# Lasting tiles in the rings, and fifteen small loads ahead of the last stores, in a matmul with bias and residual

## The chip, the cores and the metric

The kernel runs on one core of one Trainium2 chip. The metric is the time of one execution in microseconds (us).

## The reference

```python
def setup_inputs():
    batch, m, k, n = 16, 512, 1024, 768
    # x [16,512,1024], weight [1024,768], bias [768], residual [16,512,768], all float32

def reference(x, weight, bias, residual):
    return (np.matmul(x, weight) + bias + residual).astype(np.float32)
```

## The kernel before

The 8192 rows are cut into 64 row tiles of 128 rows, and eight row tiles make a super tile `S`. ACT casts a row tile of x to bf16, PE transposes it and multiplies it by the weights, POOL and DVE add bias and residual into the residual's own tile `ro`, and SP stores `ro`. All large DMAs are issued by SP, in the order of the program: SP stops at a DMA whose semaphores are not there yet, and everything behind it stops too. Buffers come from rings, which here allocate a new tile under an old tag each time:

```python
    def ring(pool, name, i, n, shape, dt):
        return pool.tile(shape, dt, name=name, tag=f"{name}{i % n}", bufs=1)
    ...
    def store(S, j0=0, j1=J, n0=0, nl=N):
        K_(nc.sync.dma_start(
            out=out_d[S, :, j0:j1, n0:n0 + nl], in_=ro[S][:, j0:j1, n0:n0 + nl]
        ))
    ...
    for t in range(HEAD, n_t):            # one row tile
        cast(t + 2)
        S, j = divmod(t, J)
        ...                               # loads of later super tiles, stores of earlier ones
        ...                               # matmuls of t, transposes of t + 1, adds of t - 1
        if S == n_s - 1 and j == 0:
            store(S - 1)                  # 3 MB
        if S == n_s - 1 and j == J // 2:
            store(S, 0, J // 2)           # 1.5 MB
        if S == n_s - 1 and j == J - 2:
            store(S, J // 2, j)           # 0.75 MB
        if S == n_s - 1 and j == J - 1:
            store(S, j - 1, j)            # 0.375 MB
    t, S = n_t - 1, n_s - 1
    for b, (n0, nl) in enumerate(chunks): # the last row tile in two parts
        ...
        store(S, J - 1, J, n0, nl)        # 0.25 and 0.125 MB
```

`S - 1` below always means the super tile before the last, `S - 2` the one before that.

Of the kernel before, what the change touches and what calls it, by code (L numbers as in the profile page):

```python
# [8 lines left out]
FP32 = mybir.dt.float32  # L9
BF16 = mybir.dt.bfloat16  # L10
P = 128
J = 8
HEAD = 3
X_BUFS = 2
RO_BUFS = 4
TMP_BUFS = 4
# [5 lines left out]
def kernel(  # L22
# [8 lines left out]
    nc = tc.nc  # L31
    x2d = x.flatten_outer_dims()
# [3 lines left out]
    N = weight.shape[1]  # L36
    n_c = K // (2 * P)
# [10 lines left out]
    const = ctx.enter_context(tc.tile_pool(name="const", bufs=1))  # L48
    sb = ctx.enter_context(tc.tile_pool(name="sb", bufs=1))
    ps = ctx.enter_context(tc.tile_pool(name="ps", bufs=1, space=bass.MemoryType.PSUM))  # L50

    def ring(pool, name, i, n, shape, dt):
        return pool.tile(shape, dt, name=name, tag=f"{name}{i % n}", bufs=1)

    def psum_o(i):
        return ring(ps, "po", i, HEAD, [P, N], FP32)

    x_sb, ro, xb, xt, po, tmp = {}, {}, {}, {}, {}, {}
    K_ = tc.keep_in_program_order


    def load_x(S, j0=0, j1=J):
        if S < n_s:
            if j0 == 0:
                x_sb[S] = ring(sb, "x_tile", S, X_BUFS, [P, J, K], FP32)
            K_(nc.sync.dma_start(out=x_sb[S][:, j0:j1, :], in_=x_d[S, :, j0:j1, :]))

    def load_res(S, j0=0, j1=J):
        if S < n_s:
            if j0 == 0:  # L70
                ro[S] = ring(sb, "ro", S, RO_BUFS, [P, J, N], FP32)
            K_(nc.sync.dma_start(out=ro[S][:, j0:j1, :], in_=res_d[S, :, j0:j1, :]))
# [4 lines left out]
# [6 lines that stand above are left out]
    def cast(t, engine="act"):  # L83
        if t < n_t:
            xb[t] = ring(sb, "xb", t, 4, [P, K], BF16)
            copy = nc.scalar.copy if engine == "act" else nc.vector.tensor_copy
            K_(copy(out=xb[t], in_=x_sb[t // J][:, t % J, :]))  # L87

    def transp(t):
        if t < n_t:  # L90

            pt = ring(ps, "pt", t, 2, [P, n_c, P], FP32)
            pairs = xb[t][:, :].bitcast(FP32)
            for c in range(n_c):
                K_(nc.tensor.transpose(  # L95
                    out=pt[:, c, :], in_=pairs[:, c * P:(c + 1) * P], identity=ident
                ))
            xt[t] = ring(sb, "xt", t, 4, [P, n_c, P], FP32)
            K_(nc.vector.tensor_copy(out=xt[t], in_=pt))  # L99
# [9 lines left out]
    def mms(t, i):  # L109
        if i == 0:  # L110
            po[t] = psum_o(t)
        for n0, nl in chunks:
            mm(t, i, n0, nl)
# [4 lines left out]
    def pool_add(t):  # L118
        if 0 <= t < n_t:
            r = row(t)  # L120
            K_(nc.gpsimd.tensor_add(out=r, in0=r, in1=tmp[t] if t < EARLY else bias_sb))  # L121

    def finish(t, n0=0, nl=N):
        if t < 0:
            return
        p = po[t][:, n0:n0 + nl]
        if t < EARLY:
            tmp[t] = ring(sb, "tmp", t, TMP_BUFS, [P, N], FP32)
            K_(nc.vector.tensor_add(out=tmp[t], in0=p, in1=bias_sb))  # L129
        else:  # L130
            K_(nc.vector.tensor_add(out=row(t, n0, nl), in0=p, in1=row(t, n0, nl)))  # L131
# [2 lines left out]
    bias_row = ring(sb, "tmp", TMP_BUFS - 1, TMP_BUFS, [P, N], FP32)  # L134
    K_(nc.gpsimd.memset(bias_row, 0.0))  # L135
    K_(nc.scalar.dma_start(out=bias_row[0:1, :], in_=bias[None, :]))
    w_st = ring(sb, "ro", RO_BUFS - 1, RO_BUFS, [P, n_c, 2, N], FP32)
    w_sb = const.tile([P, n_c, 2, N], BF16, name="w_sb")

    load_x(0, 0, 2)  # L140
# [11 lines left out]
    load_x(1, 4, 8)  # L152
    load_res(1)

    warm = const.tile([P, 512], BF16, name="warm")
    K_(nc.vector.memset(warm, 0.0))  # L156
    ones = ring(sb, "tmp", 0, TMP_BUFS, [P, P], FP32)
    K_(nc.vector.memset(ones, 1.0))
    warm_a = const.tile([1, 2], FP32, name="warm_a")
    K_(nc.vector.memset(warm_a, 0.0))  # L160
# [53 lines left out]
    for t in range(HEAD, n_t):  # L214
        cast(t + 2)
        S, j = divmod(t, J)
        if (t + 2) % J == J - 1:
            if S == 0:
                load_x(X_BUFS, 0, J // 2)
                load_x(X_BUFS, J // 2, J)  # L220
            else:
                load_x(S + X_BUFS)
            load_res(S + X_BUFS)
            if 1 <= S < n_s - 1:
                store(S - 1)
        if t < n_t - 1:
            for i in range(len(steps)):
                mms(t, i)
                if i == 0 and t >= n_t - J // 2:
                    finish(t - 1)  # L230
                if i == T_STEP:
                    transp(t + 1)
        if t < n_t - J // 2 or t == n_t - 1:
            finish(t - 1)
        if t - 1 < EARLY:
            pool_add(t - 1)
        if t + 1 >= EARLY:
            pool_add(t + 1)
        if S == n_s - 1 and j == 0:
            store(S - 1)  # L240
        if S == n_s - 1 and j == J // 2:
            store(S, 0, J // 2)
        if S == n_s - 1 and j == J - 2:
            store(S, J // 2, j)
        if S == n_s - 1 and j == J - 1:
            store(S, j - 1, j)
# [37 lines left out]
```

## Time and profile before

| | kernel before |
|---|---|
| time, median of 2 runs | 211.07 us (210.93 to 211.21) |
| span of the profiled run | 209.0 us |
| PE busy | 200.4 us, 96% |
| SP queue's packets, share of 16 DMA engines | 97.9% (87.03 MB) |
| last matmul issued | 202.8 us |
| store of S-1 issued, landed | 182.5, 200.8 us |
| the five last stores issued | 192.5 to 203.5 us |
| the five last stores landed | 204.4, 206.3, 207.2, 207.8, 208.1 us |

The landing times come from the semaphore records of the trace. First the page of the kernel before: busy time, the slices of DMA (busy tenths, then GB/s, 40 slices of 5.2 us), and the SP queue (packets, MB, share).

```profile
PE 200.4 (96%) x1274; PEld 130.6 (63%) x1299; DVE 105.0 (50%) x139; ACT 67.6 (32%) x68; POOL 115.5 (55%) x71
...
DMA  6999999999999999999999999999999999999994
GB/s 239 427 421 431 436 413 440 442 405 436 423 470 422 419 428 398 459 420 436 433 400 472 416 427 447 412 439 412 437 445 414 445 419 427 442 419 428 426 404 168
...
q1 hardware_dynamic: 5616, 87.03, 97.9%
```

PE and the DMA engines are both full. There is no slice before the last one in which the DMA engines rest, so bytes that are held up at any time have no free place later; they come out at the end.

The timeline of SP's queue from 180 us on (start, length of the merged group, what, count) shows the six stores at the end:

```profile
182.55 21.32 SPq L78 DMA_DIRECT2D out_dram<-ro  x6
```

The stores are spread over 21 us, but the last five are queued behind a store that lands at 200.8. The final 3 MB drain in 208.1 - 200.8 = 7.3 us without a pause; PE issues its last matmul at 202.8, early in that drain.

### The profile page before, as it was taken

The page shows a single profiled execution, that of the slowest core. Times are in us where ns is not written, and L with a number is a line of the kernel's source. Part 1 is how long each engine was busy: PE and PEld are TensorE (multiplying, and loading weights), DVE is VectorE, ACT ScalarE, POOL GpSimd, SP SyncE. Part 2 cuts the span into 40 slices and gives each one's busy share as a digit, 9 for nine tenths or more (in the row PEclk, how much of TensorE's full clock was granted, in tenths as well). Part 3 has the DMA queues.
Part 4 walks back from the last instruction along what each step waited for, and adds up shares of the span by engine and source line. Part 5 has one row for each costly group of instructions (what it writes and reads, how often), then busy time and mean ns, then how long its engine had stood idle before and what let it go on. Part 6 is the DMA issues. An engine that isn't in the chain of part 4 may idle for free.

```text
span 209.0 us, 3151 instructions
## 1 busy us (share of the span) xinstructions
PE 200.4 (96%) x1274; PEld 130.6 (63%) x1299; DVE 105.0 (50%) x139; ACT 67.6 (32%) x68; POOL 115.5 (55%) x71
## 2 busy tenths in 40 slices
PE   7999999999999999999999999999999999999980
PEld 2566666666666666666666666666666666666650
DVE  0737465445445544554554455455445544545550
ACT  2544315511723062422443054230724233430000
POOL 2000197819965565999189802994069910799000
PEclk9999999999999999999999999999999999999998
DMA  6999999999999999999999999999999999999994
GB/s 239 427 421 431 436 413 440 442 405 436 423 470 422 419 428 398 459 420 436 433 400 472 416 427 447 412 439 412 437 445 414 445 419 427 442 419 428 426 404 168
DMA packets 5632, 87.23 MB, mean 417 GB/s; under 512 B 625, under 2 KB 753, under 8 KB 1906
## 3 DMA queue, kind: packets, MB, share of 16 engines
q1 hardware_dynamic: 5616, 87.03, 97.9%
q8 instruction: 10, 0.16, 0.3%
q14 instruction: 4, 0.03, 0.0%
q10 hardware_dynamic: 2, 0.00, 0.0%
HBM read 61.87 MB, written 25.17 MB: 416 GB/s over the span
## 4 chain that ended last, share of the span: by engine, by line
PE 96%; issue 1%; DVE 1%
PE po L104 79%; PE pt L95 13%; PE po L170 3%; PE po L190 1%; DVE xt L99 0%; DVE ro L131 0%; DVE warm L156 0%
## 5 line engine op out<-in xcount | busy, mean ns | idle before, releaser
L104 PE MATMUL po<-w_sb,xt 128*128 128x512 bf16 (+1 forms) x999 | 175.4, 324 | 1.4
L104 PEld LDWEIGHTS <-xt 128*128 128x128 bf16 x1024 | 100.1, 98 | 59.5 <-DVE xt L99 0.5
L87 ACT CAST xb<-x_tile 128x1024 bf16<-128x1024 f32 x62 | 62.8, 1044 | 114.5 <-DMA x_tile<-in_x_dram 56.9
L121 POOL TENSOR_TENSOR ro<-ro,bias_sb 128x768 f32<-128x768 f32 x40 | 71.2, 1816 | 36.2 <-DMA ro<-in_residual_dram 26.2
L99 DVE COPY xt<-pt 128x512 f32<-128x512 f32 x64 | 44.2, 691 | 86.7 <-PE pt L95 86.5
L121 POOL TENSOR_TENSOR ro<-ro,tmp 128x768 f32<-128x768 f32 x24 | 43.1, 1814 | 41.0 <-DMA ro<-in_residual_dram 30.2
L131 DVE TENSOR_TENSOR ro<-po,ro 128x768 f32<-128x768 f32 (+2 forms) x41 | 38.0, 930 | 2.9 <-PE po L104 2.8
L95 PE MATMUL pt<-ident,xb 128*128 128x128 f32 x256 | 38.2, 273 | 0.0
L95 PEld LDWEIGHTS pt<-ident,xb 128*128 128x128 f32 x256 | 29.8, 141 | 8.1 <-issue 0.6
L129 DVE TENSOR_TENSOR tmp<-po,bias_sb 128x768 f32<-128x768 f32 x24 | 22.8, 949 | 0.6 <-POOL ro L121 0.5
L170 PE MATMUL po<-warm 128*128 128x512 bf16 x15 | 6.1, 579 | 1.2 <-DVE warm L156 1.2
L176 ACT CAST w_sb<-ro 128x768 bf16<-128x768 f32 x4 | 3.3, 832 | 4.0 <-DMA ro<-in_weight_dram 4.0
L170 PEld LDWEIGHTS <-warm 128*128 128x128 bf16 x15 | 1.9, 135 | 4.1 <-issue 2.8
L87 DVE CAST xb<-x_tile 128x1024 bf16<-128x1024 f32 x2 | 1.4, 696 | 4.8 <-DMA x_tile<-in_x_dram 4.8
L178 DVE CAST w_sb<-ro 128x768 bf16<-128x768 f32 x4 | 2.2, 555 | 2.5 <-DMA ro<-in_weight_dram 2.5
L161 ACT ACT_TABLE_LOAD x1 | 1.3, 1283 | 2.0 <-POOL ident masks.py:199 2.0
L190 PE MATMUL po<-tmp 128*128 128x512 f32 (+1 forms) x4 | 1.5, 486 | 0.0
L198 DVE COPY bias_sb<-po 128x768 f32<-128x768 f32 x1 | 1.0, 958 | 0.1
L190 PEld LDWEIGHTS po<-tmp 128*128 128x128 f32 x4 | 0.7, 190 | 0.5 <-issue 0.5
L135 POOL MEMSET tmp<- 128x768 f32 x1 | 0.7, 737 | 0.3 <-POOLq L268 0.3
L156 DVE MEMSET warm<- 128x256 uint32 x1 | 0.3, 272 | 0.9 <-PEq L268 0.9
masks.py:199 POOL TENSOR_SCALAR_AFFINE_SELECT ident<-ident 128x128 f32<-128x128 f32 x1 | 0.3, 292 | 0.1
(8 smaller groups left out, 1.0 us busy)
## 6 DMA issues: line engine op xcount, KB each, us to landing
ro<-in_residual_dram SPq DMA_DIRECT2D x7, 3072.0 KB, 18.1
out_dram<-ro SPq DMA_DIRECT2D x7, 3072.0 KB, 23.9
x_tile<-in_x_dram SPq DMA_DIRECT2D x5, 4096.0 KB, 30.8
x_tile<-in_x_dram SPq DMA_DIRECT2D x4, 2048.0 KB, 27.6
x_tile<-in_x_dram SPq DMA_DIRECT2D x3, 1024.0 KB, 8.6
ro<-in_weight_dram SPq DMA_DIRECT2D x4, 768.0 KB, 9.0
ro<-in_residual_dram SPq DMA_DIRECT2D x2, 1536.0 KB, 21.1
out_dram<-ro SPq DMA_DIRECT2D x1, 1536.0 KB, 11.9
```

What stands on the lines that cost most here:

```text
L87: K_(copy(out=xb[t], in_=x_sb[t // J][:, t % J, :]))
L95: K_(nc.tensor.transpose(out=pt[:, c, :], in_=pairs[:, c * P:(c + 1) * P], identity=ident))
L99: K_(nc.vector.tensor_copy(out=xt[t], in_=pt))
L104: K_(nc.tensor.matmul(po[t][:, n0:n0 + nl], lhsT=both[:, e, :], rhs=w_sb[:, c, e, n0:n0 + nl], start=(i == 0), stop=(i == len(steps) - 1),))
L121: K_(nc.gpsimd.tensor_add(out=r, in0=r, in1=tmp[t] if t < EARLY else bias_sb))
L129: K_(nc.vector.tensor_add(out=tmp[t], in0=p, in1=bias_sb))
L131: K_(nc.vector.tensor_add(out=row(t, n0, nl), in0=p, in1=row(t, n0, nl)))
L161: K_(nc.scalar.copy(out=warm_a, in_=warm_a))
L170: K_(nc.tensor.matmul(warm_ps[:, 0:512], lhsT=warm[:, 0:P], rhs=warm, start=True, stop=True))
L176: K_(nc.scalar.copy(out=w_sb[:, c, e, :], in_=w_st[:, c, e, :]))
L178: K_(nc.vector.tensor_copy(out=w_sb[:, c, e, :], in_=w_st[:, c, e, :]))
L190: K_(nc.tensor.matmul(bias_ps[:, n0:n0 + nl], lhsT=ones, rhs=bias_row[:, n0:n0 + nl], start=True, stop=True,))
```

## The change

It does two things. The rings hand out lasting tiles, so a buffer is no longer released and allocated again; dependencies are then tracked on the data itself. And fifteen loads of 1 to 15 rows (some 80 KB in all) into the idle warm-up tile are issued by SP ahead of the stores of the last super tile. Nobody reads what they load.

```diff
+    fixed = {}
     def ring(pool, name, i, n, shape, dt):
-        return pool.tile(shape, dt, name=name, tag=f"{name}{i % n}", bufs=1)
+        key = f"{name}{i % n}"
+        if key not in fixed:
+            fixed[key] = pool.tile(shape, dt, name=key)
+        return fixed[key]
 ... (views for w_st and ones, so that a ring has one shape; warm as 256 float32)
         if S == n_s - 1 and j == J // 2:
+            for k in range(1, 16):
+                width = 131 + 4 * k
+                K_(nc.sync.dma_start(
+                    out=warm_f[0:k, 0:width], in_=x2d[0:k, 0:width]
+                ))
             store(S, 0, J // 2)
```

More of the change, by code (lines that the diff above doesn't have):

```diff
@@ L136 @@
     K_(nc.scalar.dma_start(out=bias_row[0:1, :], in_=bias[None, :]))
-    w_st = ring(sb, "ro", RO_BUFS - 1, RO_BUFS, [P, n_c, 2, N], FP32)
+    w_st = ring(sb, "ro", RO_BUFS - 1, RO_BUFS, [P, J, N], FP32).rearrange(
+        "p (c e) n -> p c e n", e=2
+    )
     w_sb = const.tile([P, n_c, 2, N], BF16, name="w_sb")
@@ L153 @@
     load_res(1)
-    warm = const.tile([P, 512], BF16, name="warm")
+    warm_f = const.tile([P, 256], FP32, name="warm")
+    warm = warm_f[:, :].bitcast(BF16)
     K_(nc.vector.memset(warm, 0.0))
-    ones = ring(sb, "tmp", 0, TMP_BUFS, [P, P], FP32)
+    ones = ring(sb, "tmp", 0, TMP_BUFS, [P, N], FP32)[:, 0:P]
     K_(nc.vector.memset(ones, 1.0))
```

## The prediction

> **What bounds the kernel now.** Two things are full. The page: PE 96% busy, and the SP queue's packets take 97.9% of 16 DMA engines' time (87.03 MB). By the chain of waits PE sets the pace to about 203 us, one row tile per 3.04 us (timeline). The last 5 us are the store queue: the store of super tile S-1, issued at 182.5, lands at 200.8, behind the two stores before it; the five last stores (3 MB) are issued from 192.5 to 203.5 while it drains, and land at 204.4 to 208.1. So DMA never stops in the tail: 7.3 us of transfer after 200.8, then 0.8 us to the end of the span (208.97).
>
> **Lasting tiles.** The order of instructions is the same on every engine. Tile releases vanish: PE loses 122 waits on its own semaphore, and the load into x's first buffer splits its wait by half tile. In the trace PE issues at its streaming pace across those waits (a matmul start every 216 or 109 ns before and after), so they cost nothing. The earlier x load enters a DMA queue that is backlogged until 46 us. Worth: 0 ± 0.3 us.
>
> **The fifteen loads.** They write the same corner of one tile, so each waits for the landing of the one before. SP issues in order, so every store of the last super tile waits behind the chain, though its data is ready from 192 to 203. The bytes (about 80 KB) are nothing; the latency is everything.
>
> - Start: the first load is issued near 183, but its ring holds the stores of S-2 and S-1. It uses one DMA engine; the engines finish S-1 between 197.6 and 200.8 (semaphore steps). I take 198.6.
> - Step: an estimate. The trace shows 1.0 us from the first issue to its first packet and 0.35 us from a last packet to its semaphore step; [...]about 1.8 us per load (1.5 to 2.1). The Trainium skill, "DMA: Bandwidth & Descriptors", section "Anatomy of one DMA", puts a fixed cost of about 2 us on a DMA whatever its size (fitted for another issue path); the first 1 MB load here took 4.64 us, some 2.1 more than its bytes, which agrees.
> - The fifteenth is issued after 13 more landings: 198.6 + 13 × 1.8 = 222.0. No store waits for its landing.
> - Then 0.4 us of issue, a start of 2.0 us from an idle queue, 7.3 us for 3 MB, 0.8 us of end: 232.5 us of span, against 209.0.
>
> All of it is on the critical path: the last stores' overlap with PE and with the drain of S-1 is lost, and some 23 us of idle DMA queue come in.
>
> **Predicted:** span 232.5; with the 2.1 us between span and time of before, 234.6 us (11% slower), range 229 to 241. Chances: faster 0.01, same 0.03, slower 0.96.
>
> **What would show it.** SP's timeline: the first small load near 183, the second between 198 and 201, then one per 1.5 to 2.1 us whatever its rows; the last stores only after about 222, within 2 us of each other. GB/s near zero for some 23 us before them. PE's last matmul still near 203, tile pace still 3.04 us.
>
> **What would make it wrong.** A step outside 1.5 to 2.1 us (each 0.1 us is 1.3 us of time). A first load not held up by the stores in its ring: then the chain ends near 208, and the time is about 220. Lasting tiles that change PE's pace. Loads of few rows that use engines or semaphores in an unexpected way.

## The result, and the profile after

The changed kernel takes 228.39 us (median of 2 runs, 228.37 to 228.42), against 211.07. The ratio is 1.0828, with a 95% interval of 1.0802 to 1.0854. The direction was right, the mechanism too, as will be seen; the time lies 0.6 us below the predicted range of 229 to 241.

The page after, the same lines:

```profile
PE 201.6 (89%) x1299; PEld 130.5 (58%) x1299; DVE 105.0 (46%) x139; ACT 67.6 (30%) x68; POOL 115.6 (51%) x71
...
DMA  6999999999999999999999999999999999900076
GB/s 251 428 421 432 423 442 440 402 434 432 427 458 406 425 441 438 425 424 416 444 440 411 429 454 419 427 434 434 432 424 434 415 438 427 389 27 5 5 294 266
...
q1 hardware_dynamic: 5856, 87.12, 90.5%
```

PE's busy time is that of before (the counts differ by matmul records that are missing from the trace before). What is new is a hole in the DMA row: three slices at 27, 5 and 5 GB/s, then two slices in which the last stores drain. The SP queue's timeline from 180 us on shows who made it:

```profile
182.76 0.33 SPq L84 DMA_DIRECT2D out_dram<-ro_269  x1
183.19 33.02 SPq L253 DMA_DIRECT2D warm<-in_x_dram  x15
216.26 4.41 SPq L84 DMA_DIRECT2D out_dram<-ro_67  x5
```

The fifteen loads stand in SP's queue for 33 us, and the five last stores, whose data was ready from 192 to 204, are issued from 216.3 on. In the view of waits, SP's own (who waited for whom: us in total, times, longest):

```profile
SPq L253 <- DMA warm<-in_x_dram: 27.5, 14, 13.6
```

Fourteen of the loads waited for the landing of the load before. The longest wait, 13.6 us, is the second load's: the first was issued at 183.2 behind the stores of S-2 and S-1. It is one row, one packet on one DMA engine, and landed at 197.9, when those stores were through on that engine (the first of S-1's sixteen semaphore steps comes at 197.5, the last at 201.3). The other thirteen waited 27.5 - 13.6 = 13.9 us between them, 1.07 us each, and their issues come on top. The windows view gives busy times and, in the last two columns, the DMA share and GB/s of a stretch:

```profile
198.00:208.20 10.20, 5.05 (x33) 2.98 (x30) 3.24 (x5) 0.00 (x0) 0.00 (x0) 0.97 0.76 316
```

That was the drain of the kernel before; now the changed kernel:

```profile
199.30:216.30 17.00, 3.96 (x25) 2.16 (x22) 2.76 (x4) 0.00 (x0) 0.00 (x0) 0.71 0.02 7
216.30:217.40 1.10, 0.00 (x0) 0.00 (x0) 0.00 (x0) 0.00 (x0) 0.00 (x0) 0.50 0.46 189
```

For 17 us the engines are 2% busy. That is nearly all of the loss of 17.3 us. (The column before the DMA share is PE's clock; where it reads 0.50, PE's busy time is 0.00.)

Set beside the prediction, term by term, in us:

| term | predicted | measured |
|---|---|---|
| second load issued (first one landed) | 198.6 | 197.9 |
| 13 steps from the second to the fifteenth issue | 13 × 1.8 = 23.4 | 18.0 (13 × 1.383) |
| fifteenth issue to the first of the last stores | 0.4 | 0.4 |
| that store's issue to the last landing | 2.0 + 7.3 = 9.3 | 9.1 |
| last landing to the end of the span | 0.8 | 1.3 |
| span | 232.5 | 226.7 |

So 5.4 us of the 5.8 us miss in the span is one term: the step. The other terms nearly cancel.

### The profile page after: what moved, and what is told of

Read it like the earlier page. It is cut to its first block, busy times and chain, and to the rows that moved or that the text cites. A ratio compares the mean times of both kernels' runs of the same rounds, so it can differ in the third digit from the quotient of the medians.

```text
span 226.7 us, 3138 instructions
## 1 busy us (share of the span) xinstructions
PE 201.6 (89%) x1299; PEld 130.5 (58%) x1299; DVE 105.0 (46%) x139; ACT 67.6 (30%) x68; POOL 115.6 (51%) x71
## 4 chain that ended last, share of the span: by engine, by line
PE 87%; DMA 2%; DVE 1%; issue 0%
PE po_157 L110 25%; PE po_100 L110 24%; PE po_101 L110 24%; PE pt_118 L101 6%; PE pt_125 L101 6%; DMA x_tile_69<-in_x_dram 2%; PE po_101 L199 1%; DVE xb_114 L93 0%; DVE xt_208 L105 0%; PE po_100 L179 0%; DVE ro_67 L137 0%
## 5 line engine op out<-in xcount | busy, mean ns | idle before, releaser
L127 POOL TENSOR_TENSOR ro_67<-ro_67,bias_sb 128x768 f32<-128x768 f32 x16 | 28.6, 1828 | 11.7 <-DMA ro_67<-in_residual_dram 11.7
L110 PEld LDWEIGHTS <-xt_208 128*128 128x128 bf16 x256 | 25.0, 98 | 15.3 <-DVE xt_208 L105 0.5
L110 PEld LDWEIGHTS <-xt_123 128*128 128x128 bf16 x256 | 25.0, 98 | 14.8
L110 PEld LDWEIGHTS <-xt_130 128*128 128x128 bf16 x256 | 25.0, 98 | 14.8
L110 PEld LDWEIGHTS <-xt_141 128*128 128x128 bf16 x256 | 25.0, 98 | 14.7
L105 DVE COPY xt_123<-pt_118 128x512 f32<-128x512 f32 x16 | 11.1, 692 | 22.9 <-PE pt_118 L101 22.9
L105 DVE COPY xt_141<-pt_118 128x512 f32<-128x512 f32 x16 | 11.1, 692 | 21.7 <-PE pt_118 L101 21.7
L105 DVE COPY xt_130<-pt_125 128x512 f32<-128x512 f32 x16 | 11.1, 691 | 21.3 <-PE pt_125 L101 21.3
L105 DVE COPY xt_208<-pt_125 128x512 f32<-128x512 f32 x16 | 11.1, 692 | 20.7 <-PE pt_125 L101 20.6
L93 ACT CAST xb_114<-x_tile_81 128x1024 bf16<-128x1024 f32 x8 | 8.4, 1046 | 38.2 <-DMA x_tile_81<-in_x_dram 32.2
L127 POOL TENSOR_TENSOR ro_85<-ro_85,bias_sb 128x768 f32<-128x768 f32 x8 | 14.2, 1815 | 10.0 <-DMA ro_85<-in_residual_dram 10.0
L127 POOL TENSOR_TENSOR ro_269<-ro_269,bias_sb 128x768 f32<-128x768 f32 x8 | 14.3, 1831 | 10.0 <-DMA ro_269<-in_residual_dram 10.0
L110 PE MATMUL po_101<-w_sb,xt_141 128*128 128x512 bf16 x96 | 17.9, 326 | 0.0
L110 PE MATMUL po_157<-w_sb,xt_123 128*128 128x512 bf16 x96 | 17.9, 326 | 0.0
L110 PE MATMUL po_100<-w_sb,xt_130 128*128 128x512 bf16 x96 | 17.9, 326 | 0.0
L110 PE MATMUL po_157<-w_sb,xt_208 128*128 128x512 bf16 x88 | 16.5, 331 | 0.1
L127 POOL TENSOR_TENSOR ro_79<-ro_79,bias_sb 128x768 f32<-128x768 f32 x8 | 14.2, 1823 | 4.7 <-DMA ro_79<-in_residual_dram 4.7
L127 POOL TENSOR_TENSOR ro_79<-ro_79,tmp_89 128x768 f32<-128x768 f32 x2 | 3.6, 1812 | 25.2 <-DMA ro_79<-in_residual_dram 25.2
L93 ACT CAST xb_114<-x_tile_69 128x1024 bf16<-128x1024 f32 x7 | 7.3, 1046 | 29.9 <-DMA x_tile_69<-in_x_dram 21.5
L110 PE MATMUL po_100<-w_sb,xt_208 128*128 128x512 bf16 (+1 forms) x88 | 15.7, 321 | 0.0
L110 PE MATMUL po_101<-w_sb,xt_123 128*128 128x512 bf16 x80 | 14.6, 326 | 0.0
L110 PE MATMUL po_101<-w_sb,xt_130 128*128 128x512 bf16 x80 | 14.6, 326 | 0.0
```

The source lines that it names most:

```text
L93: K_(copy(out=xb[t], in_=x_sb[t // J][:, t % J, :]))
L105: K_(nc.vector.tensor_copy(out=xt[t], in_=pt))
L110: K_(nc.tensor.matmul(po[t][:, n0:n0 + nl], lhsT=both[:, e, :], rhs=w_sb[:, c, e, n0:n0 + nl], start=(i == 0), stop=(i == len(steps) - 1),))
L127: K_(nc.gpsimd.tensor_add(out=r, in0=r, in1=tmp[t] if t < EARLY else bias_sb))
```

## The experiments

Two theories stood at the start. The chain theory: fifteen latencies in a row hold up SP, which issues in order, while the DMA engines stand idle. The rivals: the lasting tiles carry part of the cost; or loads of few rows are slow or disturb the DMA engines for what follows. And one question: what a step is made of.

### Lasting tiles alone

```diff
-            for k in range(1, 16):
-                ... (the fifteen loads)
             store(S, 0, J // 2)
```

> The lasting tiles without the fifteen loads. If the loads alone cost the time: as the kernel before, 211.1 us within 0.3%, and 17.3 us under the changed kernel. If the lasting tiles carry part of the cost (rival): above 213 us. If they gain something that the loads hide: below 210.5 us.

Measured: 211.24 us against 211.5 for the kernel before; ratio 0.9996, interval 0.9981 to 1.0011. The lasting tiles cost and gain nothing, though by the prediction's count the built program loses 122 waits of PE on itself (in the trace, the separate semaphore instructions of PE's queue fall from 64 to 5).

### The loads alone, in the old rings

```diff
-    warm = const.tile([P, 512], BF16, name="warm")
+    warm_f = const.tile([P, 256], FP32, name="warm")
+    warm = warm_f[:, :].bitcast(BF16)
 ...
+            for k in range(1, 16):
+                ... (the fifteen loads)
             store(S, 0, J // 2)
```

> The fifteen loads in the kernel before, whose rings are kept as they were. If the loads alone cost the time: 228.4 us within 0.3%, with a step of about 1.38 us from one load's issue to the next, as in the changed kernel. If the lasting tiles matter (rival): away from that by over 1 us.

Measured: 228.47 us, ratio 1.0806; the mean step in its trace is 1.375 us. The whole cost sits in the loads:

```profile
183.38 32.59 SPq L245 DMA_DIRECT2D warm<-in_x_dram  x15
216.01 4.40 SPq L78 DMA_DIRECT2D out_dram<-ro  x5
```

### Each load into a place of its own

```diff
+            free = x_sb[S - 1].rearrange("p j k -> p (j k)")
+            at = 0
             for k in range(1, 16):
                 width = 131 + 4 * k
                 K_(nc.sync.dma_start(
-                    out=warm_f[0:k, 0:width], in_=x2d[0:k, 0:width]
+                    out=free[0:k, at:at + width], in_=x2d[0:k, 0:width]
                 ))
+                at += width
```

> The same fifteen loads, each into a place of its own in an x tile that is no longer needed, so that none waits for the one before; eight semaphores for DMAs make the eighth wait for the landing of the store of super tile S-1 (201.3 us). Chain theory: the stores of the last super tile are issued near 203.7 instead of 216.3, then 9.1 us of stores and 1.4 us of end: 214.1 us of span, 215.8 us of time. Rival (loads of few rows are slow in themselves, or upset the DMA engines for the stores behind them): still near 228 us, or stores that take longer than 9.1 us.

Measured: 216.19 us, ratio 1.0227; expected 215.8. The same fifteen loads of few rows cost 4.7 us instead of 17 once none waits for the one before. The timeline of SP's queue:

```profile
183.46 20.99 SPq L255 DMA_DIRECT2D x_tile<-in_x_dram  x15
204.55 4.41 SPq L84 DMA_DIRECT2D out_dram<-ro  x5
```

SP reaches the stores at 204.5. What is left is another wait, as its view of waits says; the longest one is that of the eighth load, for a landing of a store:

```profile
SPq L255 <- DMA out_dram<-ro: 11.2, 2, 6.9
```

The trace names eight DMA semaphores, used in turn, so the ninth DMA in a row needs the first one's again. The eighth load needs the semaphore of the store of S-1, so it waits until 201.5; seven more issues of some 0.4 us follow. Meanwhile the DMA engines run dry: 28% busy from 197.0 to 201.5, and 18% from 201.5 to 205.6.

### Six loads apart

```diff
-            for k in range(1, 16):
+            for k in range(1, 7):
```

(on top of the edit before)

> As the run with the loads apart (216.2 us), with six instead of fifteen. There the eighth load waited for its semaphore, which the store of super tile S-1 held until 201.5, and the DMA engines went idle from then to about 205.5. With six, the first store of the last super tile gets a semaphore that is free by 194.3 and is queued before the engines run dry: if the 4.7 us left over in that run were this wait, 211.0 to 211.6 us. If they were the loads' own cost (rival), 213 us or more (6/15 of 4.7 us and above).

Measured: 211.37 us, ratio 1.0014, interval 0.9992 to 1.0036. With six loads the first of the last stores is queued at 193.9, before the engines run dry, and nothing is lost:

```profile
183.29 6.19 SPq L255 DMA_DIRECT2D x_tile<-in_x_dram  x6
193.91 10.53 SPq L84 DMA_DIRECT2D out_dram<-ro  x5
```

By a cost per load, six would have cost 1.9 us (six fifteenths of 4.7). So the 4.7 us were the wait for a semaphore and the issues behind it, not a cost of small loads in themselves.

### A chain of seven

```diff
-            for k in range(1, 16):
+            for k in range(1, 8):
```

> Seven loads in a chain instead of fifteen (1 to 7 rows). Chain theory: eight steps of 1.38 to 1.45 us fewer, the stores are issued near 204.9, time 217.0 us. Rival (a cost of having such loads at all, once): near 228 us.

Measured: 216.84 us, ratio 1.026; expected 217.0. Eight loads fewer save 228.47 - 216.84 = 11.6 us (against the loads alone, run in the same rounds), 1.45 us each; in the trace of the changed kernel, the eight steps that are left out took 1.42 us each. The cost is by the load, not once:

```profile
183.44 21.28 SPq L253 DMA_DIRECT2D warm<-in_x_dram  x7
204.81 4.40 SPq L84 DMA_DIRECT2D out_dram<-ro  x5
```

### The chain ahead of the store of S-1

```diff
         if S == n_s - 1 and j == 0:
+            for k in range(1, 16):
+                ... (the fifteen loads, no longer at j == J // 2)
             store(S - 1)
```

> The same chain, put ahead of the store of super tile S-1 instead of behind it. If the chain begins when the ring in front of it is empty, and its cost is the DMA time that stands idle: the second load is issued near 190.6 us (when the store of S-2 is through on the first engine), the fifteenth near 208.6, then 6 MB of stores (14.6 us) and 1.5 us of start: about 226.5 us of span, 228 us of time, as the changed kernel, though all of PE's work is done before the chain ends. If the cost is the overlap of just the last stores with PE (the prediction's words): a clearly different time, over 231 or under 225 us.

Measured: 228.76 us, ratio 1.0826, the changed kernel's own. The second load is issued at 191.1, as soon as the store of S-2 is through, and the fifteenth at 209.1. The windows:

```profile
191.00:210.00 19.00, 12.39 (x81) 7.77 (x78) 7.91 (x11) 0.00 (x0) 2.72 (x2) 0.89 0.03 8
210.00:226.00 16.00, 0.00 (x0) 0.00 (x0) 0.00 (x0) 0.00 (x0) 0.00 (x0) 0.50 0.96 394
```

From the second to the fifteenth issue the chain takes 18.0 us, as in the changed kernel, with PE at work for 12.4 us of the window, and the price is the same. It is DMA time that is lost, whether PE is busy meanwhile or not. In both runs the chain goes on only when the stores queued ahead of it are through on the first load's engine: that load's packet came 13.0 us after the end of its issue in the changed kernel, and 27.8 us after it here.

### What a step is made of: one row, all rows, another source

Three runs change the loads only, at the changed kernel's place:

```diff
-                    out=warm_f[0:k, 0:width], in_=x2d[0:k, 0:width]
+                    out=warm_f[0:1, 0:width], in_=x2d[0:1, 0:width]              # one row
+                    out=warm_f[:, 0:width], in_=x2d[0:P, 0:width]                # all rows
+                    out=warm_f[0:k, 0:width], in_=x_sb[S - 1][0:k, 0, 0:width]   # from SBUF
```

> The chain of fifteen with one row each, so one DMA engine each; the widths stay. In the changed kernel's trace a step is 1.24 to 1.35 us with 3 to 7 rows and 1.44 to 1.51 us with 11 to 15. If the rows cost that (issue time and more engines to wait for): a step near 1.27 us, the stores issued 1.5 us earlier, time 226.9 us. If the step depends on something else that grows along the chain (width, time since the last store): 228.4 us.

> The chain of fifteen with 128 rows each, over all 16 engines, eight rows an engine: up to 97 KB each. If a step is mostly fixed latency: 1.5 to 1.7 us, time 230 to 233 us. If few rows are what makes these loads slow (rival): a shorter step and under 228 us.

> The chain reads from an x tile in SBUF that is no longer needed, not from x in HBM; all else equal. The prediction added 0.3 to 0.5 us of read to the 1.0 us from issue to first packet. If the read lies inside that 1.0 us (0.87 us in the chain): the time from issue to the packets shrinks by the difference between the two memories, a step of 1.0 to 1.25 us, time 223 to 227 us. If the 0.87 us are issue and descriptors alone: the step stays near 1.38 us and the time at 228.4 us.

Measured: 227.17 us with one row (ratio 1.0753), 241.65 us with 128 rows (1.1439), 238.18 us from SBUF (1.1278). The first met the estimate; the other two missed theirs, and both misses have two parts. One part is the start. In both runs the second load is issued late, at 201.7 and 201.8 instead of 197.9, as the longest wait for a load's landing shows (13.6 us in the changed kernel), first with 128 rows, then from SBUF:

```profile
SPq L253 <- DMA warm<-in_x_dram: 39.6, 14, 17.4
SPq L253 <- DMA warm<-x_tile: 31.1, 14, 17.3
```

The first load used one engine in the changed kernel. With 128 rows it used 16, and from SBUF its one row was cut into 15 packets of 36 bytes on 15 engines, so it had to wait for the stores on all or nearly all of them, and S-1's last semaphore steps come at 201.5 and 201.6. That is 3.8 and 3.9 us. The other part is the step. The trace has the time of every DMA packet, so each step can be cut at four points: the issue's start, its end, the first and the last packet of data, and the next load's issue, which waits for the landing. Means over the loads 3 to 14, in us:

| run | step | issue | issue's end to first packet | first to last packet | last packet to next issue |
|---|---|---|---|---|---|
| changed kernel (3 to 14 rows) | 1.383 | 0.276 | 0.617 | 0.138 | 0.351 |
| one row | 1.282 | 0.223 | 0.659 | 0.067 | 0.332 |
| 128 rows | 2.086 | 0.328 | 0.645 | 0.775 | 0.338 |
| from SBUF | 1.828 | 0.716 | 0.642 | 0.131 | 0.340 |

Two columns hardly move: 0.62 to 0.66 us from the issue's end to the first packet, and 0.33 to 0.35 us from the last packet to the waiting issue. From SBUF, where no HBM is read, the first packet comes no sooner. So the run gives no sign of a read of HBM in them; it can't rule out one that this run's longer issue hides. The packets take 0.03 us where one row goes alone (0.25 us in two of the twelve loads), 0.14 us for 3 to 14 rows with an engine for each, and 0.78 us for 128 rows, eight to an engine. My estimate for all rows had left out that column and the late start: with 128 rows 13 steps cost 13 × 0.70 = 9.1 us more, and the start 3.8, of the 13.3 us above the changed kernel. And the issue is part of the step. From SBUF it takes 0.72 us instead of 0.28; 13 times that difference is 5.7 us, and with the 3.9 us of the start it makes up nearly all of that run's 9.8 us. The view of this source line shows the issue (durations in ns, min/median/max), first from SBUF, then for the changed kernel:

```profile
L253 SPq DMA_DIRECT2D warm<-x_tile x15: 646/722/1149, 183.3 to 225.4; - x15
```

```profile
L253 SPq DMA_DIRECT2D warm<-in_x_dram x15: 240/273/1076, 183.2 to 215.9; - x15
```

Why the issue of an SBUF-to-SBUF copy is longer, no run here shows.

### The same chain on ACT, out of SP's way

```diff
+        if 45 <= t < 60:
+            k = t - 44
+            width = 131 + 4 * k
+            K_(nc.scalar.dma_start(
+                out=warm_f[0:k, 0:width], in_=x2d[0:k, 0:width]
+            ))
```

(and none on SP)

> The same fifteen loads, still each waiting for the one before, but issued by ACT, one for each of the row tiles 45 to 59, which are 3.04 us apart; ACT idles some 2 us of each. If the cost is a chain of latencies that blocks an in-order queue while the DMA engines stand idle: hidden here, time within 1% of the kernel before, 211 to 213 us. If loads of few rows disturb the other DMAs (rival): some us more even so. Open is how long such a load takes among full queues; over 4 us it would hold up ACT's casts, and the time would grow with it.

Measured: 220.82 us (220.38 to 223.11), ratio 1.048: my expectation missed, by the way out that it had left open. The trace gives the landing of each load. For eight of the fifteen loads, among full queues, it is 5.1 to 6.4 us after the issue; for five, where the DMA engines had gaps or had run dry, it is 1.3 to 1.6 us. With 3.04 us planned between two loads, ACT's casts stand behind the wait for the landing of the load before (waits of ACT):

```profile
ACT xb L93 <- DMA warm<-in_x_dram: 43.3, 10, 5.6
```

and PE then waits for the casts. SP's stores waited for landings of these loads too, since ACT's DMAs take their turn of the same eight semaphores (waits of SP):

```profile
SPq L84 <- DMA warm<-in_x_dram: 28.6, 3, 17.5
```

The longest of these waits held back the store of the super tile before S-2, and that of S-2 behind it, until 179.0, and from 177.0 to 179.0 the DMA engines were 5% busy and PE not at all. So the semaphores cost part of the 9.7 us; how much each of the two cost was not taken apart.

### On ACT, half as often

```diff
-        if 45 <= t < 60:
-            k = t - 44
+        if 30 <= t < 60 and t % 2 == 0:
+            k = (t - 28) // 2
```

> As the run with the loads on ACT, but one for every second row tile (30 to 58), 6.07 us apart. There a load among full queues took 5 to 6.3 us to land, more than the 3.04 us between two of them, and ACT's casts stood behind the wait. If that alone cost the 9.7 us: with 6.07 us between them the waits are over before ACT comes to them, but for a few tenths that ACT's slack takes up: 211 to 213 us. If a chain of small loads among full queues costs the other DMAs or PE something of its own (rival): 215 us or more.

Measured: 211.86 us, ratio 1.0027, interval 1.001 to 1.0044. From the second on, the loads land 5.1 to 6.4 us after their issue, as before, but the next one comes on average 6.07 us later. All fifteen loads, still in a chain, now cost 0.5 us instead of 17. Two things differ from the changed kernel, the queue and the spacing; no run spaced the loads on SP, so the share of each is not shown. The timeline of ACT shows that its waits end in time for two casts between two loads:

```profile
152.38 0.29 ACTq L251 DMA_DIRECT2D warm<-in_x_dram  x1
152.77 1.05 ACT L93 CAST xb<-x_tile 128x1024 bf16<-128x1024 f32 x1 [3.26 <-DMA warm<-in_x_dram]
154.13 1.05 ACT L93 CAST xb<-x_tile 128x1024 bf16<-128x1024 f32 x1 [0.31 <-PE pt L101]
158.32 0.30 ACTq L251 DMA_DIRECT2D warm<-in_x_dram  x1
```

No run beat the kernel before.

## Why the prediction was right or wrong

- **"Lasting tiles … worth: 0 ± 0.3 us": right.** 0.9996 in the run with them alone.
- **"Each waits for the landing of the one before … every store of the last super tile waits behind the chain": right.** Apart, the same loads cost 4.7 us; six of them apart cost nothing; a chain of seven costs what seven steps cost.
- **"Start: I take 198.6": right within 0.7 us.** The first load did queue behind the stores of S-2 and S-1, and the second was issued at 197.9.
- **"Step: about 1.8 us (1.5 to 2.1)": wrong, and the cause of the miss.** It measured 1.383 us on average, under the range too, and 13 steps make 5.4 us. The prediction had itself named a step outside its range as what would make it wrong. The sum was built from three pieces: 1.0 us from the first issue to its first packet, 0.3 to 0.5 us of read, which came from no trace, and 0.35 us from the last packet to the semaphore. The last was right (0.351). The first was taken from a load of 1 MB, whose issue alone lasted 0.377 us; a small load's issue lasts 0.276 us, so the piece is 0.276 + 0.617 = 0.89 us. And where the sum put the read, between the first and the last packet, lie 0.138 us; the run from SBUF gives no sign of a read that stands elsewhere. 0.10 us too much in the first piece and about 0.26 us in the second, with the rest from rounding up to 1.8, make the 0.42 us.
- The check against the 2.1 us fixed part of the first 1 MB load, and against the 2 us of the Trainium skill's "DMA: Bandwidth & Descriptors" (section "Anatomy of one DMA — SWDGE (gpsimd) path"), confirmed a wrong number: both hold for something else, a large load in the one case, another issue path in the other. The same page has the fitting figure elsewhere: section "Latency and other measured facts" gives about 600 ns to the first byte on the path that SP and ACT use. The trace agrees if it is counted from the end of the issue (0.62 us), and not from its start (0.89 us); the page does not say which. The page "Perfetto Trace Analysis", section "DMA Instruction — HWDGE (DVE, Sync)", says that the profiled length of a DMA issue ends when the sequencer is free again, not when data has moved; that is the 0.28 us column, so it has to be counted apart from the movement of data.
- **"All of it is on the critical path: the last stores' overlap with PE … is lost": right in size, loose in words.** With the chain moved ahead of the store of S-1 PE works through most of the hole and the time is the same. What is lost is DMA time.
- **"Then 0.4 us of issue, a start of 2.0 us, 7.3 us for 3 MB, 0.8 us of end": 9.5 us measured up to the last landing, against 9.7 before the end.** The end took 1.3 us instead of 0.8: SP's last wait ended 0.44 us after the last landing, against 0.08 us in the run with seven loads. Its cause was not looked for; it stays open.

## What to carry to other kernels

A chain of dependent small DMAs costs its number times the latency, and the bytes matter little: here 1.2 to 1.5 us a link with empty queues for up to 14 rows, 2.1 us for 128 rows, and mostly 5.1 to 6.4 us among full queues. Where an in-order queue issues it, all that stands behind it waits, and where the DMA engines are what bounds the kernel, their idle time is the price. Give such loads separate places and keep them so few that the first store behind them needs no semaphore that a long transfer still holds (six passed here, fifteen did not), or space them by more than a loaded latency on a queue that has slack; and when a latency is to be estimated, cut a load of the same size and the same issuing engine out of a trace, since a piece from a large load can belong to its size, as the issue of 0.377 us did here. Look also at how many engines the first load uses: with 15 or 16 instead of one it landed 3.8 to 3.9 us later.

## What the Trainium skill lacked or had wrong

- "DMA: Bandwidth & Descriptors" gives about 2.0 us as a DMA's fixed cost from a fit of another issue path. For small loads issued by SP with empty queues the runs show 1.28 us (one row) and 1.38 us (3 to 14 rows), made of 0.22 to 0.32 us of issue, 0.62 to 0.66 us to the first packet, the packets, and 0.33 to 0.35 us to the waiting issue.
- The same page has no figure for a small load among full queues. The runs show 5.1 to 6.4 us with the DMA engines full, issued by ACT beside SP's large transfers. Its advice that spreading DMAs over engines only saves issue time (section "Issuing engines are not separate DMA queues") leaves out that the place of issue also decides who stands behind a wait: SP's stores in the changed kernel (228.4 us), ACT's casts with the loads on ACT (220.8 us, and 211.9 us with room between them).
- No page says that the issue of a small SBUF-to-SBUF copy on SP takes longer than that of a load from HBM: 0.72 us against 0.28 us.
- No page gives the price of running out of DMA semaphores: with eight in use, the eighth of fifteen independent loads waited 6.9 us for the landing of a 3 MB store, and the kernel lost 4.7 us.
